# A softmax kernel's first load, cut into two transfers: 16 partitions at the head of the program, the other 112 behind the entry barrier

## The chip, the cores and the metric

The kernel runs on one core of one Trainium2 chip. The core has engines that work side by side: VectorE (DVE in the profile), ScalarE (ACT), GpSimd (POOL), TensorE (PE, unused here) and SyncE (SP), which only waits and issues transfers. Transfers between the chip's HBM memory and the core's on-chip memory are carried by 16 DMA engines. The on-chip memory has 128 partitions; a tile is 128 partitions by so many elements.

The metric is the device time of one execution in microseconds (us). Three runs of the kernel before took 159.79, 159.92 and 159.99 us; their median is 159.92 us.

## The reference

A softmax over the last axis of a float32 array of 16 x 1024 x 512, which is 16,384 rows of 512 numbers:

```python
def reference(x):
    x_max = np.max(x, axis=-1, keepdims=True)
    exp_x = np.exp(x - x_max)
    return (exp_x / np.sum(exp_x, axis=-1, keepdims=True)).astype(np.float32)
```

The array is 33.55 MB. It is read once and written once, 67.11 MB in all.

## The kernel before, in words

The 16,384 rows are cut into 16 groups of 1,024 rows: 8 rows on each of the 128 partitions. Two neighbouring groups make one transfer of 128 partitions by 8,192 elements (16 rows of 512), which is 32 KB a partition and 4,096 KB in all. So there are 8 loads (L0 to L7) and 8 stores (S0 to S7). The groups live in a ring of 12 places in on-chip memory; all arithmetic is done in place there. Load 6 takes the place of store 0's groups and load 7 that of store 1's, so these two wait until those stores have landed (line 197); the loads 0 to 5 wait for nothing.

Each group goes through three steps:

- M, on DVE (lines 142 to 147): wait for the group's load, then one reduction that leaves the negated maximum of each row in `stat`. MM does two groups in one instruction.
- The exponentials, on ACT (lines 149 to 155): a loop over the 16 groups; each of 8 instructions computes exp(x - max) of one row per partition and its sum.
- D or P (lines 157 to 163): DVE waits for the sums and takes their reciprocal; then DVE (D) or POOL (P) multiplies the whole group by it.

The order on DVE and POOL is written out in `SEQUENCE` (line 32): it begins M0 M1 M2 D0 M3 D1 MM4 P2 MM6 D3. The order of the transfers behind the first six loads is written out in `ORDER` (line 27): S0 S1 L6 L7 S2 S3 S4 S5 S6 S7. All 16 transfers are issued by SP, one after the other, on one DMA queue. A store waits until both of its groups are multiplied (line 170).

Every load has a semaphore of its own, `loaded[k]`. A transfer adds 16 to its semaphore when it has landed, and line 144 waits for 16.

The first six loads are issued in the loop at lines 175 to 177. A program begins with an entry barrier among all engines, and its main block stands ahead of the kernel's body. The function `loads_at_the_head` (lines 41 to 57) takes the first transfers of SP out of the body and puts them into the main block ahead of SP's part of that barrier. `AT_HEAD` (line 37) says how many: one. So load 0 is the program's first instruction on SP, and loads 1 to 5 follow behind the barrier.

Of the kernel before, what the change touches and what calls it, by code (L numbers as in the profile page):

```python
# [21 lines left out]
GROUPS = sum(LOADS)  # L22
LOAD_AT = [sum(LOADS[:k]) for k in range(len(LOADS))]
STORE_AT = [sum(STORES[:k]) for k in range(len(STORES))]

ORDER = """
S0 S1 L6 L7 S2 S3 S4 S5 S6 S7
# [33 lines left out]
def kernel(  # L61
# [5 lines left out]
    nc = tc.nc  # L67
    nc.at_finalize(loads_at_the_head)
    P = nc.NUM_PARTITIONS

    x_rows, out_rows = x.flatten_outer_dims(), out.flatten_outer_dims()
# [11 lines left out]
    def sem(name):  # L83
        return ctx.enter_context(nc.semaphore(name))

    maxima, summed, inverted = [sem(s) for s in ("maxima", "summed", "inverted")]
    loaded = [sem(f"loaded{k}") for k in range(len(LOADS))]
    scaled = [sem(f"scaled{k}") for k in range(len(STORES))]

    def load_of(g):  # L90
        return max(k for k in range(len(LOADS)) if LOAD_AT[k] <= g)

    def store_of(g):
        return max(k for k in range(len(STORES)) if STORE_AT[k] <= g)

# [11 lines left out]
    def at(g):  # L107
        return g % RING

    def rows(g, groups=1):  # L110
        part = ring[:, at(g) * GROUP * d : (at(g) + groups) * GROUP * d]
        return part.rearrange("p (r d) -> p r d", d=d)

    def cols(t, g, groups=1):
        return t[:, at(g) * GROUP : (at(g) + groups) * GROUP]

    def in_dram(t, g, groups):
        k = load_of(g)
        assert load_of(g + groups - 1) == k
        part = t[P * GROUP * LOAD_AT[k] : P * GROUP * (LOAD_AT[k] + LOADS[k]), :]  # L120
        first = (g - LOAD_AT[k]) * GROUP
        part = part.rearrange("(p r) d -> p r d", p=P)
        return part[:, first : first + groups * GROUP, :]

    def load(k):
        g, n = LOAD_AT[k], LOADS[k]
        return nc.sync.dma_start(out=rows(g, n), in_=in_dram(x_rows, g, n))

    def store(k):
        g, n = STORE_AT[k], STORES[k]  # L130
        return nc.sync.dma_start(out=in_dram(out_rows, g, n), in_=rows(g, n))
# [9 lines left out]

    def rowmax(g, groups):
        assert load_of(g) == load_of(g + groups - 1)
        nc.vector.wait_ge(loaded[load_of(g)], 16)  # L144
        nc.vector.reduce_max(  # L145
            out=cols(stat, g, groups), in_=rows(g, groups), axis=AX, negate=True
        ).then_inc(maxima, groups)
# [25 lines left out]

    with tc.manual_schedule(engines={SP}):
        for k in range(min(before)):
            first = load(k).then_inc(loaded[k], 16)
            tc.info.no_tile_sem_insts.add(first.ins.name)
    tc.close()
    tc.compile()  # L179

# [2 lines left out]
    for work in SEQUENCE.split():  # L183
        kind = work.rstrip("0123456789")
        g = int(work[len(kind) :])
        if kind in ("M", "MM"):
            rowmax(g, len(kind))
        else:
            scale(g, nc.vector if kind == "D" else nc.gpsimd)
    for transfer in ORDER.split():  # L190
        k = int(transfer[1:])
        if transfer[0] == "S":
            store_scaled(k)
        else:
            last = before[k]
            since = max([a for a in awaited if a < last], default=-1)
            nc.sync.wait_ge(stored[last], 16 * (last - since))
            load(k).then_inc(loaded[k], 16)
# [32 lines left out]
```

## Time and profile before

| what | value |
| --- | --- |
| median of three runs | 159.92 us (159.79 to 159.99) |
| the profiled execution, its own time | 160.08 us |
| its span, first to last instruction | 158.8 us |
| outside of the span (160.08 - 158.76) | 1.3 us |
| DMA queue: time of its packets, as a share of 16 engines' span | 98.9% |
| mean rate of the transfers | 423 GB/s |
| DVE busy | 121.8 us (77%) |
| ACT busy | 92.2 us (58%) |
| POOL busy | 42.3 us (27%) |
| issue of load 0 on SP | at 0.00, 0.38 us long |
| issue of load 1 on SP, behind the barrier | at 0.79 us |
| first packet of load 0 starts | at 1.04 us |
| load 0 landed | at 12.34 us |
| last store issued, landed | at 137.84 us, 158.73 us |

A transfer is carried as packets. The trace has 2,304 of them for 16 transfers, which is 144 a transfer: 128 packets of 32 KB, one for each partition, and 16 of 4 bytes that tell of the landing, one from each DMA engine. So each DMA engine carries 8 packets of 32 KB of each transfer. The trace's packet records hold start, length and size of each; they do not name the engine. Away from the start of the program a 32 KB packet takes 1.213 us (median of 2,048).

Times in the trace count from the first instruction of the program, which is the issue of load 0. The busy share of an engine is a mean over the whole span; what a change at the start is worth is read from the start, and from what the start is followed by.

### The profile page before, as it was taken

How to read it: one execution, taken by the hardware profiler on the slowest of the kernel's cores; microseconds unless marked ns; L12 is line 12 of the kernel's file. 1: busy time of each engine (PE TensorE's matmuls, PEld its weight loads, DVE VectorE, ACT ScalarE, POOL GpSimd, SP SyncE). 2: the span in 40 equal slices, each digit the busy share in tenths (PEclk: the TensorE clock that was granted, in tenths of full speed). 3: DMA queues.
4: the chain of work that ended last, by engine and by line, in shares of the span. 5: the costliest groups of instructions: out<-in, count | busy, mean ns of one | idle time of the engine just before them, and what ended most of it. 6: DMA issues, size and time to landing. Idle time of an engine off the chain costs nothing.

```text
span 158.8 us, 572 instructions
## 1 busy us (share of the span) xinstructions
DVE 121.8 (77%) x36; ACT 92.2 (58%) x257; POOL 42.3 (27%) x10
## 2 busy tenths in 40 slices
DVE  0008979999999999999999499999999999700000
ACT  0300699969406999999988990899599300000000
POOL 0000000000007903930970790079049300000000
DMA  7999999999999999999999999999999999999996
GB/s 264 438 479 405 405 495 421 396 438 471 413 405 438 471 405 396 396 413 471 438 396 462 446 413 405 454 421 438 438 421 446 413 446 438 438 421 438 429 429 264
DMA packets 2304, 67.11 MB, mean 423 GB/s; under 512 B 256, under 2 KB 256, under 8 KB 256
## 3 DMA queue, kind: packets, MB, share of 16 engines
q1 hardware_dynamic: 2304, 67.11, 98.9%
HBM read 33.55 MB, written 33.55 MB: 423 GB/s over the span
## 4 chain that ended last, share of the span: by engine, by line
DMA 45%; DVE 39%; issue 2%; DVEq 0%
DMA ring<-in_x_dram 26%; DVE ring L161 22%; DMA out_dram<-ring 20%; DVE stat L145 16%; DVE recip L159 1%; DVEq L144 0%
## 5 line engine op out<-in xcount | busy, mean ns | idle before, releaser
L134 ACT ACTIVATE ring<-ring,stat x128 | 90.4, 707 | 28.1 <-ACTq L151 28.1
L145 DVE TENSOR_REDUCE stat<-ring 128x16 f32<-128x8192 f32 (+1 forms) x10 | 69.5, 6956 | 15.7 <-DMA ring<-in_x_dram 15.7
L161 POOL TENSOR_TENSOR ring<-ring,recip 128x4096 f32<-128x4096 f32 x6 | 42.1, 7016 | 81.8 <-DVE recip L159 81.8
L161 DVE TENSOR_TENSOR ring<-ring,recip 128x4096 f32<-128x4096 f32 x10 | 51.1, 5109 | 0.3
L134 ACT ACTIVATION_READ_ACCUMULATOR ring<-ring,stat x128 | 23.8, 186 | 0.0
L181 ACT ACT_TABLE_LOAD x1 | 1.3, 1283 | 4.0 <-PEq L179 4.0
L159 DVE RECIPROCAL recip<-stat 128x8 f32<-128x8 f32 x16 | 3.0, 190 | 0.0
L215 POOL MEMSET const-float32-0.0<- 128x1 f32 x1 | 0.1, 98 | 0.2 <-issue 0.2
L215 POOL MEMSET const-bfloat16-1.0<- 128x1 bf16 x1 | 0.1, 102 | 0.0
L215 POOL MEMSET const-uint8-127<- 128x1 uint8 x1 | 0.1, 102 | 0.0
L215 POOL MEMSET const-float32-1.0<- 128x1 f32 x1 | 0.1, 98 | 0.0
## 6 DMA issues: line engine op xcount, KB each, us to landing
ring<-in_x_dram SPq DMA_DIRECT2D x8, 4096.0 KB, 25.9
out_dram<-ring SPq DMA_DIRECT2D x8, 4096.0 KB, 24.0
```

The costliest lines, as they stand in the source:

```text
L134: return nc.scalar.activation(out=row, in_=row, func=EXP, bias=one, scale=1.0, accum_out=one)
L145: nc.vector.reduce_max(out=cols(stat, g, groups), in_=rows(g, groups), axis=AX, negate=True).then_inc(maxima, groups)
L159: nc.vector.reciprocal(out=cols(recip, g), in_=cols(stat, g)).then_inc(inverted, 1)
L161: engine.tensor_mul(out=rows(g), in0=rows(g), in1=spread(cols(recip, g))).then_inc(scaled[store_of(g)], 1)
L181: nc.scalar.preload_act_table(EXP)
L215: nc = _bacc.Bacc("TRN2", target_bir_lowering=False, num_devices=1)
```

## The change

Load 0 becomes two transfers with the same bytes in the same places: the partitions 0 to 15, and the partitions 16 to 127. Each adds 16 to `loaded[0]`, so the maxima of groups 0 and 1 wait for 32 in place of 16. `AT_HEAD` stays at one, so the transfer of 16 partitions stands ahead of the entry barrier, and the one of 112 partitions stands behind it, ahead of load 1. SP issues 17 transfers in place of 16; the instructions of the other engines are the same, in the same order.

```diff
+FIRST = 16
...
-    def load(k):
+    def load(k, first=0, last=P):
         g, n = LOAD_AT[k], LOADS[k]
-        return nc.sync.dma_start(out=rows(g, n), in_=in_dram(x_rows, g, n))
+        return nc.sync.dma_start(
+            out=rows(g, n)[first:last], in_=in_dram(x_rows, g, n)[first:last]
+        )
...
-        nc.vector.wait_ge(loaded[load_of(g)], 16)
+        nc.vector.wait_ge(loaded[load_of(g)], 32 if load_of(g) == 0 else 16)
...
         for k in range(min(before)):
-            first = load(k).then_inc(loaded[k], 16)
-            tc.info.no_tile_sem_insts.add(first.ins.name)
+            at_partition = [0, FIRST, P] if k == 0 else [0, P]
+            for first, last in zip(at_partition, at_partition[1:]):
+                issued = load(k, first, last).then_inc(loaded[k], 16)
+                tc.info.no_tile_sem_insts.add(issued.ins.name)
```

## The prediction

> **What bounds the kernel now.** I read the page's engine shares first, then its DMA rows, then the share of the DMA engines in four long stretches, and last the start of the program, which is where the change lies.
>
> ```profile
> DVE 121.8 (77%) x36; ACT 92.2 (58%) x257; POOL 42.3 (27%) x10
> ...
> DMA  7999999999999999999999999999999999999996
> ...
> q1 hardware_dynamic: 2304, 67.11, 98.9%
> HBM read 33.55 MB, written 33.55 MB: 423 GB/s over the span
> ```
>
> The 16 DMA engines are busy for 98.9% of the span, and of 40 slices only the first and the last are not full. The busiest compute engine has 23% to spare. So the time is: until the first packet starts, then 128 packets of 32 KB on each DMA engine without a pause, then the landing.
>
> ```profile
> 12.00:52.00 40.00, 38.63 (x11) 25.93 (x73) 3.28 (x1) 1.00 1.00 433
> 52.00:92.00 40.00, 37.55 (x13) 38.84 (x111) 21.35 (x4) 1.00 0.99 421
> 92.00:132.00 40.00, 39.86 (x12) 26.19 (x74) 17.47 (x3) 1.00 1.01 433
> 132.00:158.70 26.70, 5.77 (x3) 0.00 (x0) 0.00 (x0) 1.00 0.95 409
> ```
>
> The columns are stretch, length, busy DVE, ACT and POOL, clock, DMA share, GB/s. The DMA share is 0.95 to 1.01 in every stretch, the middle one included, where loads and stores alternate. DVE is nearly full from 12 to 132 us too, but its work is there to be waited for by SP, and SP is early: the last store is issued at 137.84 us, while the store two before it lands at 139.39 and the one before it at 149.08. The queue holds about 11 us of work when the last store joins it. A late start of the DMA stream therefore moves everything behind it by the same amount, and the end too.
>
> The start, in short stretches and in order of time:
>
> ```profile
> 0.00:1.00 1.00, 0.00 (x0) 0.00 (x0) 0.20 (x4) 1.00 0.00 0
> 1.00:1.50 0.50, 0.00 (x0) 0.00 (x0) 0.00 (x0) 1.00 3.68 983
> 1.50:2.50 1.00, 0.00 (x0) 0.00 (x0) 0.00 (x0) 1.00 0.08 33
> 2.50:3.00 0.50, 0.00 (x0) 0.00 (x0) 0.00 (x0) 1.00 0.46 197
> 3.00:3.50 0.50, 0.00 (x0) 0.00 (x0) 0.00 (x0) 1.00 2.02 852
> ```
>
> ```profile
> 0.00 3.17 SPq L127 DMA_DIRECT2D ring<-in_x_dram  x6
> ...
> 3.97 1.28 ACT L181 ACT_TABLE_LOAD   x1 [3.97 <-PEq L179]
> 12.37 8.74 DVE L145 TENSOR_REDUCE stat<-ring 128x8 f32<-128x4096 f32 x2 [12.37 <-DMA ring<-in_x_dram]
> ```
>
> A stretch here is charged with a packet where the packet starts, so a share can pass 1. Between 1.0 and 1.5 us 983 GB/s x 0.5 us / 32,768 bytes = 15 packets start; one more starts at 1.69. That is one on each engine. Their mean length is 3.68 x 0.5 x 16 / 15 = 1.96 us against 1.213 later. Then nothing starts until 2.78 us: the second packet on an engine begins when its first is done (the first of them starts at 2.78, where the earliest first packet ends). Whatever holds up the first packet holds up the other 127 of that engine.
>
> **The change part by part.**
>
> 1. The transfer at the head. It was 128 partitions, 8 packets an engine; it is now 16 partitions, 16 packets. I take them to lie one on each of the 16 engines, as both 16 and 112 divide by 16; rival C is the other case. Count: 1 + 7 = 8 packets an engine, as before. The bytes on an engine do not change.
>
> 2. Its issue. SP's issue of 128 partitions takes 0.33 to 0.52 us, load 0's 0.383. One for 16 partitions takes between 0 and 0.52 us, so the barrier behind it moves by -0.38 to +0.14 us. I take 0, by the nearest row, 0.383. The first packets may also start sooner or closer together: they start from 1.04 to 1.69 us now, so 0 to 0.65 us could be had. I take 0, as 15 of the 16 start within 0.31 us of the first, and keep -0.65 as an end.
>
> 3. The issue behind the barrier. SP issues one transfer more, 0.33 to 0.52 us. The 112 partitions are issued at about 0.79 us, where load 1 was; by load 0's row their packets can start 1.04 us later, at 1.83 us. The engines are free for them at 2.78 at the earliest, so 0.95 us cover this (0.4 us, were the first packets to take 1.213 from 1.04). Loads 1 to 5 are issued 0.33 to 0.57 us later (last one from 2.70 to about 3.2); load 1's first packet is wanted when load 0 is done, near 12 us. The barrier behind the loads moves from 3.9 to about 4.4 us, and so does ACT's table load at 3.97; ACT's first exponential starts at 17.14 us. POOL waits until 48.72 us. All of this costs 0 behind a cover of at least 8 us.
>
> 4. The second landing. 16 more packets of 4 bytes, 9 ns each, one an engine: +0.01 us. A boundary between transfers costs no more than this now: the last engine lands load 0 at 12.34, load 1 at 22.03, load 2 at 31.74, steps of 9.69 to 9.71 against 8 x 1.213 + 0.009 = 9.71.
>
> 5. The wait for 32. DVE's first reduction stands at the head of its queue behind this wait. With both parts landed when 8 packets an engine are done it ends where it did, 12.37 us. If they land later, DVE, then ACT, then S0 (issued 39.96, wanted near 60 us) all move, with 20 us to spare.
>
> 6. The pace of the packets. This is the one unknown that lies on the path, and it decides the sign. In all 16 transfers of the trace, 128 partitions are in flight and each engine has eight of them as its own; 32,768 bytes / 1.213 us = 27.0 GB/s is the pace of an engine, and equally the pace of its eight partitions. Which of the two sets it, the trace cannot say, since they always go together. The change takes them apart: for the first time 16 engines work on 16 neighbouring partitions.
>  - Fast end: the engine sets the pace. 16 partitions take one packet time, and the sum is 0.
>  - Slow end: the partitions set it, eight sharing 27.0 GB/s. 16 partitions are two eights and take 8 x 1.213 = 9.70 us in place of 1.21: +8.5 us, in which the engines' packets of the other 112 wait in line behind. The 112 are 14 eights on 16 engines: 8 x 1.213 in place of 7 x 1.213, +1.2 us. Together +9.7 us.
>  - No row is nearer to one end than to the other: the nearest, a whole transfer, fits both. I take the middle, +4.9 us. It is what four shared paths in place of two would make of it: 4 x 1.213 = 4.85 us for the first packets, 3.6 more, and the 1.2 of the 112.
>
> [...]
>
> **Sum.** Steps 1 to 5: 0.0 us. Step 6: +4.9 us, all at the start, passed on one for one to the end. On the profiled execution, 160.08 + 4.9 = 165.0 us; that execution is 0.16 us over the median of 159.92, so the forecast against the median is 164.8 us.
>
> **The rivals.** What this kernel's measurement can tell from no change is about 0.2%, 0.32 us.
>
> A. *The partitions set no pace* (fast end). For it: behind the first 16, only 35 of 2,032 packets take over 1.244 us, the longest 2.07. Against it: there engine and partitions are always paired one to one. The time is 159.9 us, within 0.3 us.
>
> B. *Faster: the short first transfer starts its packets sooner.* It needs A, and then step 2's gain: descriptors for 16 rows in place of 128. For it: the first packets start 1.04 us after the issue begins and spread over 0.65 us. Against it: no row shows that this delay grows with the partitions, and the 112 must be in place by the time the first packets end. The gain is at most 0.65 us, 159.3 us; it decides once more than half of that, 0.32 us, is had without any loss in step 6.
>
> C. *The 16 partitions stay with the engines that own them in whole transfers.* Then a few engines carry them, the others start with the 112 at about 1.83 in place of 1.04 us, and every engine has its 8 packets as before. The time is 159.9 + 0.4 to 0.8 = 160.5 us. For it: whole transfers show a fixed eight an engine. Against it: 16 divides by 16.
>
> D. *The 112 collide as well.* Handed out as 1, 17, 33 and so on, each step of the 112 falls on 16 neighbours like the head. Seven packets at the middle price, 4 x 1.213, cost 7 x 3.64 = 25.5 us more on top of 3.6: 189 us. For it: nothing says how 112 are dealt out. Against it: in whole transfers an engine's eight do not collide with the others'.
>
> **How the numbers follow.** The forecast case (a loss of 2 to 10.5 us by step 6) has 0.62; its own range is 162 to 170.5 us. D has 0.10. C has 0.05. A has 0.08 and B 0.15. Faster is B, 0.15; the same is A, 0.08; slower is the rest, 0.77. The range 159.5 to 170.5 takes in the forecast, A, C and the smaller half of B; it leaves out D and the larger gains of B, under 2 in 10. It is wide, because the two ends of step 6 are 9.7 us apart.
>
> **What would show it.** In the changed kernel the stretch from 1.0 to 1.5 us still starts some 15 or 16 packets, but their mean length is several us in place of 1.96, and the next packets start near 5 to 7 us in place of 2.78. DVE's first reduction starts at 14 to 22 us in place of 12.37. From then on the steps between loads are 9.7 us again, the DMA share is 0.95 to 1.01, DVE, ACT and POOL keep their busy times, and the span is longer by what the first reduction is late. If second packets start before 3.2 us and the reduction by 12.4, step 6 is wrong and A or B holds. If there is a hole in the DMA share between first and second packets with first packets of 2 us, it is the cover in step 3 that failed. If DVE's first reduction is late by over 20 us, D holds.

## The result, and the profile after

The changed kernel takes 168.87 us, the median of six runs (168.21 to 168.94); beside it the kernel before took 159.93 us (159.79 to 159.99). The ratio is 1.0552 with a 95% interval of 1.0538 to 1.0565: slower by 8.94 us. The forecast was 164.8 us, in a range of 159.5 to 170.5. The profiled execution took 168.21 us, its span is 166.9 us; it is the fastest of the six, so the traces differ by 8.1 us where the medians differ by 8.9.

The page of the changed kernel, DMA rows. The two strings have one figure for each of 40 slices of 4.17 us: busy share in tenths, and GB/s.

```profile
DMA  9989999999999999999999999999999999999996
GB/s 141 236 251 251 251 471 393 424 456 393 487 393 479 393 416 456 401 479 393 479 401 463 408 416 448 408 456 401 479 401 463 408 424 448 416 456 408 471 401 267
...
q1 hardware_dynamic: 2320, 67.11, 99.0%
```

The DMA engines are as busy as before, 99.0% against 98.9%, and that is the trap of this profile: in the first five slices they are busy at 141 to 251 GB/s, and at 393 to 487 in all others but the last. A DMA engine counts as busy while its packet is under way, however slowly. What changed is the pace of the first 4 MB, not the share. The same in longer stretches of the changed kernel (stretch, length, busy DVE, ACT, POOL, clock, DMA share, GB/s):

```profile
1.00:3.50 2.50, 0.00 (x0) 0.00 (x0) 0.00 (x0) 1.00 1.44 210
3.50:20.00 16.50, 0.00 (x0) 1.28 (x1) 0.00 (x0) 1.00 1.00 248
20.00:30.00 10.00, 8.57 (x2) 3.80 (x11) 0.00 (x0) 1.00 0.98 419
30.00:70.00 40.00, 38.98 (x12) 31.09 (x89) 7.02 (x1) 1.00 1.00 432
```

From 3.5 to 20 us the 112 partitions come in at 248 GB/s; behind them, up to 70 us, the transfers run at 419 to 432, the pace of before. The first stretches and the instructions of the start:

```profile
1.00:1.50 0.50, 0.00 (x0) 0.00 (x0) 0.00 (x0) 1.00 7.22 1049
1.50:2.50 1.00, 0.00 (x0) 0.00 (x0) 0.00 (x0) 1.00 0.00 0
2.50:3.00 0.50, 0.00 (x0) 0.00 (x0) 0.00 (x0) 1.00 0.00 0
3.00:3.50 0.50, 0.00 (x0) 0.00 (x0) 0.00 (x0) 1.00 0.00 0
```

```profile
0.00 3.50 SPq L129 DMA_DIRECT2D ring<-in_x_dram  x7
...
4.29 1.28 ACT L187 ACT_TABLE_LOAD   x1 [4.29 <-PEq L185]
21.43 4.42 DVE L149 TENSOR_REDUCE stat<-ring 128x8 f32<-128x4096 f32 x1 [21.43 <-DMA ring<-in_x_dram]
```

1049 GB/s x 0.5 us / 32,768 bytes = 16 packets start in the first stretch, one on each engine; they take 7.22 x 0.5 = 3.61 us each, where they took 1.92 before. DVE's first reduction starts at 21.43 us in place of 12.37.

The trace's packet records give the sum, per DMA engine: the first packet takes 3.61 us in place of 1.92 (+1.7), the seven of the 112 partitions take 2.13 in place of 1.217 each (+6.4), load 1's first packet 1.74 in place of 1.21 (+0.5), and the other 119 give back 0.5. That is 165.0 us of packets in place of 156.9, which is the 8.1 us between the spans. **Most of the loss lies in the 112 partitions, not in the 16.** In the records each packet starts within 0.06 us of the end of another, and so they line up as 16 chains, as many as there are engines: none of them is without a packet while the 112 come in.

### The profile page after: what moved, and what is told of

The parts are those of the page before. It is cut to its first block, busy times and chain, and to the rows that moved or that the text cites. A ratio compares the mean times of both kernels' runs of the same rounds, so it can differ in the third digit from the quotient of the medians.

```text
span 166.9 us, 573 instructions
## 1 busy us (share of the span) xinstructions
DVE 121.8 (73%) x36; ACT 92.2 (55%) x257; POOL 42.3 (25%) x10
## 4 chain that ended last, share of the span: by engine, by line
DMA 48%; DVE 37%; issue 2%; SPq 0%; DVEq 0%
DMA ring<-in_x_dram 30%; DVE ring L165 21%; DMA out_dram<-ring 18%; DVE stat L149 16%; DVE recip L163 1%; SPq L129 0%; DVEq L148 0%
## 5 line engine op out<-in xcount | busy, mean ns | idle before, releaser
L138 ACT ACTIVATION_READ_ACCUMULATOR ring<-ring,stat x128 | 24.3, 190 | 0.0
```

The source lines that it names most:

```text
L138: return nc.scalar.activation(out=row, in_=row, func=EXP, bias=one, scale=1.0, accum_out=one)
```

## The experiments

Four explanations were held against each other. PATHS: the partitions written set the pace, as if neighbouring ones shared a path (the author's supposition; no trace here shows a path). SHAPE: 16 and 112 are bad counts. TWO: a second transfer at the start costs in whatever form. START: the part behind the barrier comes too late. A fifth, SOURCE, puts the collision on the side of HBM. All ratios below are against the kernel before on the same chip.

### Both parts ahead of the barrier

```diff
-AT_HEAD = {mybir.EngineType.SP: 1}
+AT_HEAD = {mybir.EngineType.SP: 2}
```

> Both parts of load 0 stand ahead of the entry barrier, otherwise as the changed kernel. Theory PATHS (16 neighbouring partitions are reached over fewer paths than 16 engines can fill, and shares of 7 neighbours collide as well): the place of the barrier does not matter, 168.9 us within 0.4, first reduction at about 21.4 us. Rival START (the part behind the barrier comes too late and the engines run dry): the time falls back to 160 to 161 us and the first reduction to 12.4 us.

Measured: 168.82 us against 159.97, ratio 1.0556 (1.0537 to 1.0575), first reduction at 21.92 us. The place of the barrier has no part in it, and START falls. The changed kernel's own records say the same: the first packet of the 112 starts at 3.74 us, when the first of the 16 ends, and they had been issued at 0.81.

### A cut at 64

```diff
-FIRST = 16
+FIRST = 64
```

> Load 0 is cut at 64 partitions in place of 16, so both parts have 64 partitions, a power of two, 4 packets of 32 KB an engine each. PATHS, with eight partitions to a path: each half has only 8 of 16 paths, 8 x 1.213 = 9.7 us in place of 4.85, and the two in turn cost about +9.7 us, 169.6 us (between 166 and 171, as the halves may overlap at the seam). Rival SHAPE (16 and 112 are bad counts, a count that divides 128 evenly is not): 160 to 161 us. Rival TWO (a second transfer at the start costs whatever its form): 168 to 169 us.

Measured: 170.12 us, ratio 1.063 (1.0614 to 1.0646), first reduction at 23.56 us: +10.15 us where PATHS said +9.7. SHAPE falls in the form that only uneven counts are slow. This run is the longest of the cuts of load 0 that were tried. The single transfers below go the same way: 12.6 us for 64 partitions alone, where the whole 128 take 12.3, and 7.3 for 32.

### A cut along the rows

The same two transfers of 512 and 3,584 KB at the same two places, but each with all 128 partitions.

```diff
-FIRST = 16
+FIRST = 2
...
-            out=rows(g, n)[first:last], in_=in_dram(x_rows, g, n)[first:last]
+            out=rows(g, n)[:, first:last], in_=in_dram(x_rows, g, n)[:, first:last]
...
-            at_partition = [0, FIRST, P] if k == 0 else [0, P]
+            at_row = [0, FIRST, 2 * GROUP] if k == 0 else [0, 2 * GROUP]
...
```

With 2 rows at the head:

> Load 0 is cut along the rows of each partition: 2 of 16 rows of all 128 partitions at the head (512 KB, packets of 4 KB), 14 rows of all 128 behind the barrier (packets of 28 KB). Bytes, number and place of the transfers are those of the changed kernel; only no part has fewer than 128 partitions. PATHS: every engine keeps its eight partitions, so the loss is gone, 159.5 to 160.5 us, first reduction at 12.2 to 12.9 us. TWO or START: the loss stays, 168 to 169 us. It also tells what is to be had from a short first transfer: nothing, if it lies within 0.3 us of 159.9.

Measured: 160.13 us, ratio 1.0019 (1.0000 to 1.0037). The trace of this kernel, instructions and stretches in which load 0 arrives:

```profile
0.00 3.57 SPq L129 DMA_DIRECT2D ring<-in_x_dram  x7
...
12.31 8.75 DVE L149 TENSOR_REDUCE stat<-ring 128x8 f32<-128x4096 f32 x2 [12.31 <-DMA ring<-in_x_dram]
```

```profile
2.50:11.00 8.50, 0.00 (x0) 1.28 (x1) 0.00 (x0) 1.00 1.06 451
```

SP still issues seven transfers, and yet the first reduction starts at 12.31 us and the pace is 451 GB/s where it was 248. So TWO falls: number, bytes, place and barrier are those of the changed kernel, and the loss is gone. What is left of it is the cut across the partitions.

With 1 row at the head:

> As the cut along the rows, with 1 row of all 128 partitions at the head (256 KB, packets of 2 KB) and 15 behind the barrier. The head's packets are done within about 1 us; if the second part's packets start only 1.04 us after its issue at 0.8, at 1.84, the engines idle for a few tenths. PATHS: 159.5 to 160.5 us. If the length of the first packets (1.96 us where 1.213 is usual) is a fixed delay paid once per program, a shorter first packet pays it under the head's transfer and 0 to 0.7 us could be gained; 159.3 us would be its best.

Measured: 160.23 us, ratio 1.0039 (1.0007 to 1.0071). A shorter first transfer gains nothing in the whole: the first reduction starts at 12.65 us in place of 12.37. No version tried here beats the kernel before.

### The same cut in load 3

```diff
+SPLIT = 3
...
-        nc.vector.wait_ge(loaded[load_of(g)], 32 if load_of(g) == 0 else 16)
+        nc.vector.wait_ge(loaded[load_of(g)], 32 if load_of(g) == SPLIT else 16)
...
-            at_partition = [0, FIRST, P] if k == 0 else [0, P]
+            at_partition = [0, FIRST, P] if k == SPLIT else [0, P]
```

> Load 0 is whole again and load 3, in the middle of the first six loads with a full queue ahead of it and behind it, is cut into 16 and 112 partitions. PATHS: the same bytes collide in the same way, so the same loss at another place: 168 to 169 us, the landing of load 3 about 9 us later than 41.45, the loads 0 to 2 as before. START (loss only where the pipeline fills): 160 to 160.5 us.

Measured: 169.12 us, ratio 1.0562 (1.0544 to 1.0581). The stretch from 31 to 50 us, first of this kernel, then of the kernel before:

```profile
31.00:50.00 19.00, 17.48 (x5) 10.03 (x29) 1.40 (x1) 1.00 0.99 231
```

```profile
31.00:50.00 19.00, 18.97 (x7) 10.07 (x29) 1.28 (x1) 1.00 1.00 433
```

Loads 0 to 2 land as before (load 1 at 21.90 us), then 4 MB take 19 us at 231 GB/s with the DMA share at 0.99. The loss is the same, 9.2 us, in a place with a full queue on both sides. It belongs to the cut, not to the start of a program.

### Each part as an additional transfer

The kernel before with load 0 whole and behind the barrier, and one additional transfer at the head into load 5's place.

```diff
+        ahead = nc.sync.dma_start(
+            out=rows(10, 2)[0:16], in_=in_dram(x_rows, 10, 2)[0:16]     # or [:, 0:2], or [16:128]
+        ).then_inc(extra, 16)
...
-        for k in range(min(before)):
+        for k in range(min(before) - 1):
...
+    nc.sync.wait_ge(extra, 16)
+    load(5).then_inc(loaded[5], 16)
```

> Load 0 is whole, behind the barrier; at the head stands an additional transfer of 16 partitions x 32 KB into the place of load 5, which load 5 overwrites once it has landed (these bytes are read twice). Priced by rows: 1.21 us for the bytes, and what 16 neighbouring partitions lose. By the landings of the changed kernel and of the cut along the rows (6.56 against 3.81 us for 512 KB) the loss is 2.75: 163.9 us. By the prediction's term of 3.6: 164.8. If 16 partitions lose nothing by themselves and only the 112 do: 161.2 us.

> The control: the same additional 512 KB at the head, as 2 rows of all 128 partitions. Nothing but the bytes to pay, 1.21 us: 161.2 us within 0.4.

> The additional transfer at the head is the other part, partitions 16 to 127 (3,584 KB, 7 packets an engine), without the 16 ahead of it. The bytes cost 7 x 1.213 = 8.5 us. If the 112 lose by themselves what the landings of the changed kernel say (14.85 us for them against 8.47 for 14 rows of 128 partitions), 6.4 us more: 174.8 us. If they lose only the prediction's 1.2: 169.6. If they lose because the 16 ahead throw the engines out of step: 168.5.

| additional transfer | time | over 159.96 | the bytes at full pace | left |
| --- | --- | --- | --- | --- |
| 16 partitions, 512 KB | 163.74 us | 3.78 | 1.21 | 2.6 |
| 128 partitions x 2 rows, 512 KB | 161.31 us | 1.35 | 1.21 | 0.1 |
| 112 partitions, 3,584 KB | 173.99 us | 14.03 | 8.49 | 5.5 |

The control of 2 rows rests on four runs of which one took 163.36 us, so its ratio of 1.013 has an interval of 1.0053 to 1.0207, and by the times alone its verdict is unclear. The packet records of the profiled runs decide it: per DMA engine, the packets take 1.17 us more than in the kernel before with the 2 rows, 3.62 with the 16 partitions and 13.58 with the 112; the spans are 159.7, 162.5 and 172.6 us against 158.8. Less the bytes at full pace that leaves 0.0, 2.4 and 5.1 us.

Both parts lose by themselves, and the larger one loses twice as much: it needs no 16 ahead of it to throw the engines out of step. 2.6 + 5.5 = 8.1 of the 8.9 us. The intervals of the two ratios put this sum between 7.1 and 8.9, so the remaining 0.8 is hardly beyond the noise, and no cause is shown for it.

### Single transfers, one at a time

Two kernels issue transfers one by one ahead of all else, each when the one before has landed; they have 32 KB a partition where nothing else is said. Each transfer was timed once; the whole 128 partitions, which stand in both kernels, took 12.3 us both times. The first:

```diff
...
+    probe(1, nc.sync.dma_start(out=spare[0:16], in_=source[0:16]))
+    probe(2, nc.sync.dma_start(out=spare[16:128], in_=source[16:128]))
+    probe(3, nc.sync.dma_start(out=spare[0:16], in_=source[0:128:8]))
+    probe(4, nc.sync.dma_start(out=spare[0:128:8], in_=source[0:16]))
...
```

> Ahead of the loads, twelve transfers are issued one by one, each when the one before has landed, into a place of the ring that load 5 later overwrites; load 0 is not at the head. Its time is no measure of the change; read is each transfer's time from issue to landing. [...] Rival SOURCE (neighbouring blocks of HBM collide): the spread source into partitions 0-15 falls to about 4, and the neighbouring source into every eighth partition stays at 6.5 to 7.5. Rival SHAPE: 64 partitions 7.5 us, 32 partitions 5.0. [...]

Its instructions on SP: start and length of each issue. A transfer's time is the next one's start less its own.

```profile
1.39 0.38 SPq L193 DMA_DIRECT2D ring<-in_x_dram  x1
13.68 0.35 SPq L194 DMA_DIRECT2D ring<-in_x_dram  x1
19.98 0.31 SPq L195 DMA_DIRECT2D ring<-in_x_dram  x1
37.66 0.31 SPq L196 DMA_DIRECT2D ring<-in_x_dram  x1
44.30 0.56 SPq L197 DMA_DIRECT2D ring<-in_x_dram  x1
48.86 0.32 SPq L198 DMA_DIRECT2D ring<-in_x_dram  x1
56.13 0.48 SPq L199 DMA_DIRECT2D ring<-in_x_dram  x1
68.71 0.47 SPq L200 DMA_DIRECT2D ring<-in_x_dram  x1
81.39 0.32 SPq L201 DMA_DIRECT2D ring<-in_x_dram  x1
98.24 0.32 SPq L202 DMA_DIRECT2D ring<-in_x_dram  x1
114.83 0.31 SPq L203 DMA_DIRECT2D ring<-in_x_dram  x1
121.24 0.35 SPq L204 DMA_DIRECT2D ring<-in_x_dram  x1
```

| line | written partitions | read blocks | us |
| --- | --- | --- | --- |
| L193 | 0-127 | 0-127 | 12.3 |
| L194 | 0-15 | 0-15 | 6.3 |
| L195 | 16-127 | 16-127 | 17.7 |
| L196 | 0-15 | every eighth | 6.6 |
| L197 | every eighth | 0-15 | 4.6 |
| L198 | 0-31 | 0-31 | 7.3 |
| L199 | 0-63 | 0-63 | 12.6 |
| L200 | 64-127 | 64-127 | 12.7 |
| L201 | 0-95 | 0-95 | 16.8 |
| L202 | 0-111 | 0-111 | 16.6 |
| L203 | 48-63 | 48-63 | 6.4 |
| L204 | 0-127, 4 KB each | 0-127 | 3.4 |

SOURCE falls for the 16 partitions: reading 256 KB apart does not help partitions 0 to 15 (6.6 us), but writing to every eighth partition does (4.6). For the 112 the reading side was not varied by itself. The same 512 KB take 6.3 us over 16 neighbours and 3.4 over 128 partitions. Half the partitions take as long as all of them, 12.6 and 12.7 us against 12.3. And 112 partitions take 17.7 us where 128 take 12.3: **fewer bytes, 5.4 us more**. The author's estimates for 96 and 112 partitions were too low; 16.6 to 17.7 us were measured.

The second lays four and eight partitions in different ways, and has other counts and the other direction:

```diff
...
+    probe(2, nc.sync.dma_start(out=spare[0:4], in_=source[0:4]))
+    probe(3, nc.sync.dma_start(out=spare[0:16:4], in_=source[0:4]))
+    probe(4, nc.sync.dma_start(out=spare[0:128:32], in_=source[0:4]))
...
+    probe(11, nc.sync.dma_start(out=target[0:16], in_=spare[0:16]))
...
```

> Fourteen single transfers, each issued when the one before has landed; the time is no measure of the change, read is issue to landing. [...] One partition: some 3.3 us, which is the fixed part and one packet. [...] Counts: 48 about 9, 80 about 14, 120 no faster than 128, 14 to 18, since only whole 128 keep the fixed eights. Stores: the same side of the chip, so 16 partitions 6 to 7 us, 64 as long as 128, and 112 longer than 128.

From its instructions on SP, read as above: one partition (L195), 0-3, then 0, 4, 8, 12, then 0, 32, 64, 96, then 0-7, every fourth of 0-31 (L200), then 48, 80 and 120 partitions (L201 to L203); from L204 on they are stores, of which L206 is that of partitions 16-127.

```profile
13.66 0.31 SPq L195 DMA_DIRECT2D ring<-in_x_dram  x1
16.64 0.25 SPq L196 DMA_DIRECT2D ring<-in_x_dram  x1
22.86 0.71 SPq L197 DMA_DIRECT2D ring<-in_x_dram  x1
26.51 0.52 SPq L198 DMA_DIRECT2D ring<-in_x_dram  x1
31.18 0.28 SPq L199 DMA_DIRECT2D ring<-in_x_dram  x1
37.51 0.67 SPq L200 DMA_DIRECT2D ring<-in_x_dram  x1
41.13 0.33 SPq L201 DMA_DIRECT2D ring<-in_x_dram  x1
55.13 0.31 SPq L202 DMA_DIRECT2D ring<-in_x_dram  x1
69.31 0.33 SPq L203 DMA_DIRECT2D ring<-in_x_dram  x1
91.22 0.38 SPq L204 DMA_DIRECT2D out_dram<-ring  x1
...
108.75 0.32 SPq L206 DMA_DIRECT2D out_dram<-ring  x1
121.32 0.54 SPq L207 DMA_DIRECT2D out_dram<-ring  x1
```

One partition takes 2.98 us. Four neighbours take 6.22, four that stand 4 apart 3.65, four that stand 32 apart 4.67. Eight neighbours take no longer than four, 6.33, and eight that stand 4 apart 3.62. So the same number of partitions takes from 3.65 to 6.22 us, or from 3.62 to 6.33, by where they lie. What the neighbours share, and where on the way, no trace shows.

| transfer alone | us from issue to landing |
| --- | --- |
| load, 48 partitions | 14.0 |
| load, 80 partitions | 14.2 |
| load, 120 partitions | 21.9 |
| store, 128 partitions | 11.1 |
| store, 16 partitions | 6.4 |
| store, 64 partitions | 11.9 |
| store, partitions 16-127 | 12.5 |

Two of the expectations missed: 48 partitions were expected at about 9 and take 14.0 us, more than 64, and 120 were expected at 14 to 18 and take 21.9.

Which partitions an engine gets no trace shows. What the records of the changed kernel show is the number of the packets and their length: those of partitions 16 to 127 line up as 16 chains of 7, and they take 2.13 us each, where the seven in their place before took 1.217.

**For the count of this change the loss is measured and not explained.** Alone, the whole 128 take 12.3 us, of which 8 x 1.213 = 9.7 are packets at full pace and 2.6 lie around them. An estimate from these numbers for the 112, with 7 packets an engine at the same pace, is 8.5 + 2.6 = 11.1 us; 16.6 to 17.7 were measured for 112 partitions. The store of partitions 16 to 127 takes 12.5 us, 1.4 us more than that of 128. What slows the load slows the one store of this shape that was timed far less.

## Why the prediction was right, and where its size was off

The sign and the place were forecast, and that the 16 partitions lose (their packets took 3.61 us, the first ones of before 1.92). The size was about half of what came, +4.9 against +8.94 us, and most of what came lies in the other part, the 112.

- **Step 1** held: 16 packets start together, one on each engine. Rival C falls with it.
- **Step 2** held at its value of 0: the issue of 16 partitions takes 0.389 us, that of 128 took 0.383, and the first packets start at 1.03 to 1.38 us. Rival B's gain does not exist; both cuts along the rows, which have no loss to hide it, lie at or above the time of before.
- **Step 3** held: the 112 were issued at 0.81 us and the first engine was free for them at 3.74, the last load is issued at 3.06 us, the table load moved from 3.97 to 4.29 and nobody waited for it.
- **Step 4**: the 4-byte packets of this seam took 0.035 us in place of 0.009. Nothing.
- **Step 5** held: S0 is issued at 49.01 us in place of 39.96, the last store at 146.17 in place of 137.84, and the landings between show no new gap.
- **Step 6** is the term that was mis-sized, in both of its parts. The 16 partitions were priced at +3.6 us, as 4 x 1.213 in place of 1.213. No run shows the four shared paths behind this term; what the runs showed in its place is 2.6 us as an additional transfer, and 1.7 by packet lengths. A part of this stood in the prediction's own rows: the first packets took 1.92 us before, not 1.213. The 112 were priced at +1.2 us, as 14 eights in place of 16; no run shows that eight partitions share a pace, and the 112 lose 5.5 as an additional transfer and 6.4 in the kernel. All 16 engines have packets under way from 3.5 to 20 us, and yet 248 GB/s come in, which is the pace of about nine engines at 27.0. What holds them up no trace shows. The slow end, +9.7, put 8.5 of it on the 16 and was right in its sum by luck.
- **Rival A** is excluded by the control of the rows. **D** is excluded by its size, 25.5 us for the 112 where 5.5 to 6.4 were measured. But its first sentence, that the 112 collide as well, is what the forecast lacked, and the larger part of the loss.

In the changed kernel the 16 packets at the head take 4.2 us from the first start to the last end, 124 GB/s, and a transfer of these 512 KB alone takes 6.3 us from issue to landing, 83 GB/s.

One thing stays open above all: why a load of partitions 16 to 127 takes 5.4 us more than one of 128 where a store takes 1.4 more (12.5 against 11.1). The sign and the place of the loss are shown by the controls; the cause of its size is not shown by any run.

## What to carry to other kernels

If a transfer has to be cut, cut it along the rows of each partition and not across the partitions: here the same 512 + 3,584 KB cost 0.2 us one way and 8.9 the other. Where the DMA bounds a kernel, read GB/s beside the busy share, since a DMA engine counts as busy while its packet is under way: a share of 1.00 went with 248 GB/s from 3.5 to 20 us and with 432 from 30 to 70. And before pricing a transfer of a new shape by its bytes, time it alone: 48, 80, 96, 112 and 120 partitions all took longer than 128, 14.0 to 21.9 us against 12.3.

## What the runs showed of the hardware that was not expected

The time of a load is not monotonic in its partitions: 12.3 us for 128, 12.6 for 64, but 14.0 for 48, 14.2 for 80, 16.8 for 96, 16.6 to 17.7 for 112 and 21.9 for 120, at 32 KB each. The worst of those tried is the count nearest to 128. A smaller transfer is hardly issued faster: alone it takes SP 0.25 to 0.39 us for most counts from 1 to 128 partitions, and 0.47 to 0.71 us for 64 partitions and where strided partitions are written.
